# A list scheduler of two MLPs: transfers share one bus in the plan

## The chip, the core and the metric

The kernel runs on one core of a Trainium2 chip. A core has five engines that each carry out their own list of instructions in order: TensorE (PE in the rows; PEld is its loading of weights), VectorE (DVE), ScalarE (ACT), GpSimd (POOL) and SyncE (SP), which here only issues transfers between HBM and the on-chip memory. They wait for one another through semaphores. The metric is the device time of one execution in microseconds.

## The reference, cut to what matters

Two layers over 1024 latent tokens and 256 context tokens of width 1024, all in float32. Layer 0 is windowed attention, layer 1 a gated linear recurrence ("the middle" below); each is followed by a dense MLP:

```
def sqrelu_mlp(h, w1, w2):
    return jnp.square(jax.nn.relu(h @ w1)) @ w2

x = x + mx[2] * rms_norm(y_x, g[1])                       # after the mixer
x = x + mx[5] * rms_norm(sqrelu_mlp(modulate(rms_norm(x, g[2]), mx[3], mx[4]), mlp_w1[i], mlp_w2[i]), g[3])
```

Context tokens go through layer 0's MLP too, not through layer 1's. `mx` are six rows of modulation for each layer, the product of SiLU(c) with `ada_w`. w1 is 1024 x 4096, w2 is 4096 x 1024.

## The kernel before

Float32 products are made of three matmuls on split operands: each operand is a high part, rounded by a cast (line 236), and the remainder (lines 1371, 1465, 1517, 1585); high by high, high by low and low by high are added in a PSUM bank (lines 241 to 243). So each weight or activation tile is loaded, cast and subtracted before TensorE can use it.

The tokens are three groups: 0 and 1 are 512 latent tokens each (tiles 0 to 3 and 4 to 7), 2 is the context (tiles 8 and 9). Layer 0's MLP (`layer0_mlp`) begins with four weight tiles of w1 (`plan_w`, lines 1505 to 1521) by the plain product: the normalized tiles `xn` are loaded, transposed on TensorE (line 1571, tile `ph`), modulated and split (lines 1575 to 1585, tiles `h` and `hf`), then multiplied (`pf`), squared and stored. From then on two weight tiles and both latent groups are done at once by a scheme with seven products in place of eight (`plan_seven`; fourteen steps in layer 0). In a step, TensorE makes p1, p6, p5, p7, p2, p4 and p3 of twelve matmuls each, in banks `al`, `be`, `de`, `ga`; line 1419 (ScalarE) copies p1, line 1421 adds p6, line 1424 adds p7 in bank `ga` and line 1425 p5; p4 adds on in `ga` and p3 in `de`, so they wait for lines 1424 and 1425. Lines 1430 and 1431 make the last two results, lines 1435 and 1437 square them, and they are stored in HBM (`hid_d`). The weights of a step are prepared one step ahead: line 1381 (`s`) and line 1357 are differences and sums of weight blocks, which GpSimd or VectorE can do.

In the second phase (`plan_second`) the hidden tiles are read back and multiplied with w2 in chunks of four hidden tiles (first chunk: two); results are copied (first chunk) or added on (line 1492). Beside layer 0's MLP the modulation rows of the next layer are made on VectorE: a load of 512 KB of `ada_t` (`raw`), and for each one or two products with accumulation (line 1227, operands `raw` and `srow`); when the eight of a row are there, lines 1237 and 317 finish it, and a gate row is then transposed on TensorE (line 325, `gt`).

What sets the order is a planner, the class `Plan`. Each stage adds its operations with an engine (or several to choose from), a duration, a key, what they depend on and which buffers they take and free. `order` goes through them greedily: for each engine it takes the operation with the lowest key among those that can begin about first, on the times that the plan itself keeps, and picks among engines that may do the same work by when they would be done. A transfer is planned with a fixed duration from its issue, any number at once: 2800 ns for a weight tile, 2500 for a tile of activations, 2300 for a store, 3000 for a gate row. `emit` then writes the instructions out in order of planned times, and each engine follows that order on the chip, however long things take there. `KEYS3` holds the numbers of both MLPs; the middle has its own, `KEYS2`, in which there is a key `bw=9` already, for another use. The attention stage's planner uses `KEYS`, the projections `KEYS0`.

Of the kernel before, what the change touches and what calls it, by code (L numbers as in the profile page):

```python
# [42 lines left out]
class Plan:  # L43
# [19 lines left out]
    def any(self, table, order, key, fn, deps=(), take=(), free=(), tab=None):  # L63
        order = order.split()
        return self.add(order, [table[e] for e in order], key, fn, deps, take, free, tab)
# [12 lines left out]
    def order(self):  # L78
        ops = self.ops
        users = [[] for _ in ops]  # L80
        wait = [len(o[3]) for o in ops]
        for i, o in enumerate(ops):
            for d in o[3]:
                users[d].append(i)
        ready = [[] for _ in ops]
        end = {e: self.start.get(e, 0.0) for e in self.LAT}
        open_ = {e: [] for e in self.LAT}
        free = self.free
        tab = None
        for i, o in enumerate(ops):  # L90
            if not wait[i]:
                for e, ns in o[0]:
                    open_[e].append(i)
        at = []
        eps = self.keys["eps"]
        pen = self.keys.get("tab", 0)
        slack = self.keys.get("alt", 0)

        def first(i, e):
            o = ops[i]  # L100
            t = max([end[e]] + [f + self.lat(q, e) for f, q in ready[i]])
            for s in dict.fromkeys(o[4]):
                k = o[4].count(s)
                if len(free[s]) < k:
                    return None
                f = free[s][k - 1]
                t = max(t, f[0] + self.lat(f[1], e))
            return t
        while len(at) < len(ops):
            best = None  # L110
            for e, c in open_.items():
                ts = []
                for i in c:
                    t = first(i, e)
                    if t is None:
                        continue
                    o = ops[i][0]
                    if len(o) > 1 and o[0][0] != e:
                        if t + dict(o)[e] > first(i, o[0][0]) + o[0][1] + slack:
                            continue  # L120
                    ts.append((t, i))
                if not ts:
                    continue
                lim = min(ts)[0] + eps.get(e, 0)
                k, t, i = min((ops[i][1] + (pen if ops[i][6] not in (None, tab) else 0), t, i) for t, i in ts if t <= lim)
                if best is None or t < best[0]:
                    best = t, i, e
            if best is None:
                raise RuntimeError("plan is stuck: " + str([(ops[i][0], ops[i][1], ops[i][4]) for c in open_.values() for i in c]))
            t, i, eng = best  # L130
            opts, key, fn, deps, take, fr, tb, _ = ops[i]
            for e, ns in opts:
                open_[e].remove(i)
            self.got[i] = [(s, free[s].pop(0)[2]) for s in take]
            f = t + dict(opts)[eng]
            if tb is not None and tb != tab and eng == "ACT":
                tab = tb
                f += 1283
            if eng != "DMA":
                end[eng] = f  # L140
            for x in fr:
                s, q = (x, None) if isinstance(x, str) else self.got[x[0]][x[1]]
                free[s].append((f, eng, q))
                free[s].sort(key=lambda x: x[0])
            at.append((t, i, eng, f))
            for u in users[i]:
                ready[u].append((f, eng))
                wait[u] -= 1
                if not wait[u]:
                    for e, ns in ops[u][0]:  # L150
                        open_[e].append(u)
        self.span = max(f for t, i, eng, f in at)
        return at
# [37 lines left out]
class Body:  # L191
    KEYS = {'ctx': 0.706, 'kv': 0.956, 'q': -1.4, 'S': -0.826, 'dS': 0.182, 'v': 0.068, 'e': 0.292, 'n': -0.211, 'tp': 0.197, 'dt': 0.205, 'a': 0.087, 'pv': 0.593, 'o': 0.343, 'w': 0.695, 'dw': 0.162, 'r': 0.664, 'eps': {'ACT': 143.51971938059006, 'Pool': 265}}
    KEYS0 = {'cr': 32.6, 'x': [2.69, 4.49, -4.04, -3.82, 11.07, 11.46, 13.54, 8.52, 59.28, 46.73], 'a0': 6.01, 'ad': 4.7, 'ac': 7.11, 'cp': [1, 0, 0, 0, 1, 1, 0, 1, 1, 1, 1, 1, 0, 1, 0, 0], 'w': [2.18, 62.63, 75.38], 'wd': [13.74, 0.3, 15.36], 'h': [-24.73, 13.55, 40.24], 'hd': [3.18, 5.2, 4.18], 'tl': 19.32, 'blocks': [[[0, 1, 2, 3, 4, 5], [6, 7], [8, 9]], [[0, 1, 2], [3, 4], [5, 6], [7, 8, 9]], [[8, 9, 0], [1], [2], [3]]], 'cq': [1, 0, 0, 1, 0, 1, 0, 1, 1, 1, 1, 0, 0, 0, 0, 1, 1, 0, 1, 1, 0, 1, 1, 1], 'p': [32.68, -6.89, 47.14, 3.71, 20.15, -8.8, 64.94], 'pd': 7.27, 'p1': 82.17, 'qk': -8.12, 'k': 144.05, 'g': [45.38, 61.79, 109.14], 'gd': [5.61, 8.84, 15.66], 'alt': 1800, 'eps': {'Q': 0, 'PE': 0, 'Pool': 44, 'DVE': 27, 'ACT': 0}}
    KEYS3 = dict(r=3, alt=200, eps=dict(DVE=100))
    KEYS2 = dict(m=(2.3, 0.68, 10.54), p=(7.5, 1.52, 9.72), h=(10.4, 11.24, 37.3), pi=0.66, a0=28.64, ap=9.33, al=-5.36, g0=155.5,
                 g1=151.7, gp=4.73, c0=98.5, cp=2.33, w0=312.9, wp=16.6, r0=389.52, spill=5, tab=122.87, alt=72.5, ba=8, bb=6, bw=9, bg=7,
                 bo=0, hm=1, eps=dict(DVE=20, ACT=0, Pool=48))
# [948 lines left out]
    def layer0_mlp(self):  # L1146
        nc, A = self.nc, self.A
        U, l = 4, 0
        dma = nc.sync.dma_start
        p = Plan(self.places(), self.KEYS3, start=dict(PE=9000.0, DVE=5000.0, ACT=5000.0))  # L1150
        self.srow = [None, None]
# [112 lines left out]
    def mlp(self, l, S):  # L1264
# [3 lines left out]
        slots["t"] = [(q, 1) for q in S["free"] + sum(S["hold"], [])]  # L1268
        p = Plan(slots, self.KEYS3)
        hold = [[(p.hold("t", q), 0) for q in v] for v in S["hold"]]  # L1270
# [10 lines left out]


    def plan_second(self, p, l, K, m, n, c, put, last, ys, yop, yh, order, rows=None, fin=False):
        nc, A = self.nc, self.A
        hid, w2, hc = [], [], []
# [12 lines left out]
        for i, t in enumerate(order):  # L1298
# [14 lines left out]
            if fin:  # L1313
                def load(pool, t=t):
                    xs[t] = pool.tile([P, D], F32, tag="x", name=self.name("x"))
                    nc.sync.dma_start(out=xs[t], in_=self.x_d[2, t])
                xop[t] = p.add("DMA", 2500, K, load, [nxt], take=["t"])
                self.plan_residual(p, K + 2 * i + self.KEYS3["r"], t, ys, yop[t], xs, xop[t], G, lambda t, c: nc.sync.dma_start(
                    out=self.out[t, :, c], in_=xs[t][:, c]), False)
# [886 lines left out]
```

## Time and profile before

| | us |
|---|---|
| median of 3 runs (2899.05 to 2900.18) | 2899.95 |
| the profiled execution | 2898.64 |
| its span | 2896.9 |
| TensorE busy in the span | 2685.5 (93%) |
| VectorE busy | 2103.5 (73%) |
| ScalarE busy | 1134.6 (39%) |
| GpSimd busy | 916.2 (32%) |

The attention ends at about 670 us. Layer 0's MLP has its start up to 765, the seven-product steps to 1117 and the second phase to 1525; the middle goes to about 2236, layer 1's MLP has its steps to 2531 and its second phase to 2878, and the rest is the end. Times are from the start of the span. In a row of a timeline the number in brackets is the time for which the engine stood idle just before, and behind the arrow stands what released it. The granted clock (PEclk) is 1.00 at 2.4 GHz and 0.50 at 1.2 GHz.

### The profile page before, as it was taken

Reading aid. Unit: us, or ns where it says so; the run is one execution under the profiler, and the core shown is the slowest. Engines: PE = TensorE matmul, PEld = TensorE weight load, DVE = VectorE, ACT = ScalarE, POOL = GpSimd, SP = SyncE. Lnnn points to the kernel's source line nnn. Section 1 sums busy time; section 2 is a strip of 40 time slices with the busy share of each in tenths; the row PEclk is TensorE's granted clock in tenths of the full one; section 3 lists DMA queues with packets and bytes.
Section 4 is the critical chain, followed back from the end, with each engine's and each line's share of the span. In section 5 each row is a group of like instructions: output and inputs, shape, how many; then the busy total and the mean of one; then the engine's idle time right before and its main releaser. Section 6 shows DMA issues by size and latency. Waiting matters only on the chain.

```text
span 2896.9 us, 35250 instructions
## 1 busy us (share of the span) xinstructions
PE 2685.5 (93%) x12886; PEld 2209.1 (76%) x12886; DVE 2103.5 (73%) x3085; ACT 1134.6 (39%) x2106; POOL 916.2 (32%) x753
## 2 busy tenths in 40 slices
PE   6888999999999999999997998987698999999997
PEld 4676787887788888888885886775576888888886
DVE  8988999996866665655547658689979767655546
ACT  5326777774322223112105335686616222231111
POOL 7653444443311112211106102145628322211113
PEclk9899999999999999999998998998899999999999
DMA  6462321124233335444433213243342233333323
GB/s 235 161 209 92 105 67 59 55 66 167 84 106 113 109 124 176 148 142 138 150 123 145 99 66 109 98 145 125 112 149 95 93 112 117 131 117 116 102 80 123
DMA packets 115332, 345.03 MB, mean 119 GB/s; under 512 B 12836, under 2 KB 15828, under 8 KB 115160
## 3 DMA queue, kind: packets, MB, share of 16 engines
q1 hardware_dynamic: 111704, 330.21, 33.9%
q10 hardware_dynamic: 3456, 12.58, 1.1%
q8 instruction: 101, 1.65, 0.2%
q14 instruction: 71, 0.58, 0.1%
HBM read 254.37 MB, written 88.38 MB: 118 GB/s over the span
## 4 chain that ended last, share of the span: by engine, by line
PE 58%; DVE 18%; issue 8%; ACT 4%; POOL 3%; DMA 2%; SPq 0%; ACTq 0%; DVEq 0%; POOLq 0%
PE py L242 9%; PE py L243 9%; PE py L241 9%; PE pf L243 7%; PE pf L241 7%; PE pf L242 7%; DVE x L1633 2%; PE py L1084 2%; PE tp L1001 1%; PE pv L1015 1%; DVE gi L2079 1%; DVE sc L971 1%; DMA raw<-in_ada_t 1%; DVE gi L2071 1%; PE pq L861 1%
## 5 line engine op out<-in xcount | busy, mean ns | idle before, releaser
L241 PE MATMUL pf<-h,w 128*128 128x512 f32 (+1 forms) x1400 | 520.2, 372 | 23.2 <-DVE c L1424 8.9
L243 PE MATMUL pf<-h,w 128*128 128x512 f32 (+1 forms) x1400 | 518.2, 370 | 13.7 <-DVE w L1517 6.8
L242 PE MATMUL pf<-h,w 128*128 128x512 f32 (+1 forms) x1400 | 518.2, 370 | 7.4 <-DVE h L1585 7.4
L1492 DVE TENSOR_TENSOR y<-y,py 128x512 f32<-128x512 f32 x268 | 180.2, 682 | 258.8 <-PE py L243 258.8
L241 PEld LDWEIGHTS pf<-h,w 128*128 128x128 f32 x1400 | 269.7, 193 | 71.2 <-DVE c L1424 11.4
L243 PEld LDWEIGHTS pf<-h,w 128*128 128x128 f32 x1400 | 269.4, 192 | 60.0 <-POOL w L1517 8.4
L242 PEld LDWEIGHTS pf<-h,w 128*128 128x128 f32 x1400 | 269.5, 193 | 52.9 <-DVE h L1585 10.9
L236 ACT CAST w<-raw 128x1024 fp32r<-128x1024 f32 x132 | 138.4, 1048 | 421.1 <-DMA raw<-in_w 189.2
L236 ACT CAST hw<-raw 128x512 fp32r<-128x512 f32 x159 | 94.1, 620 | 366.0 <-PE py L243 132.1
L241 PE MATMUL py<-hw,hw 128*128 128x512 f32 x608 | 236.6, 389 | 0.8 <-DVE y L1492 0.8
L242 PE MATMUL py<-hw,hw 128*128 128x512 f32 x608 | 236.5, 389 | 0.0
L243 PE MATMUL py<-hw,hw 128*128 128x512 f32 x608 | 236.5, 389 | 0.0
L1465 POOL TENSOR_TENSOR hw<-raw,hw 128x512 fp32r<-128x512 f32 x60 | 90.0, 1507 | 416.3 <-DVE hw L236 257.4
L241 PE MATMUL py<-w,hw 128*128 128x512 f32 x416 | 164.2, 395 | 13.1 <-DVE y L1673 13.1
L995 POOL TENSOR_SCALAR P<-P,sc 128x640 f32<-128x640 f32 (+2 forms) x160 | 118.4, 752 | 179.7 <-DVE sc L992 94.0
L243 PE MATMUL py<-w,hw 128*128 128x512 f32 x416 | 163.3, 393 | 0.0
L242 PE MATMUL py<-w,hw 128*128 128x512 f32 x416 | 163.3, 393 | 0.0
L1084 PE MATMUL py<-w,oT 128*128 128x512 f32 x480 | 146.6, 410 | 2.8 <-DVE w L919 2.1
L1465 DVE TENSOR_TENSOR hw<-raw,hw 128x512 fp32r<-128x512 f32 x144 | 116.2, 837 | 26.4 <-ACT hw L236 26.1
L978 ACT ACTIVATE P<-S,sc 128x640 f32<-128x640 f32 (+2 forms) x160 | 113.9, 712 | 52.7 <-DVE sc L972 37.1
L241 PEld LDWEIGHTS py<-hw,hw 128*128 128x128 f32 x608 | 114.1, 188 | 24.9 <-DVE y L1492 1.3
L243 PEld LDWEIGHTS py<-hw,hw 128*128 128x128 f32 x608 | 114.1, 188 | 23.7
(295 smaller groups left out, 6440.4 us busy)
## 6 DMA issues: line engine op xcount, KB each, us to landing
raw<-in_w SPq DMA_DIRECT2D x128, 512.0 KB, 4.1
raw<-in_ada_t SPq DMA_DIRECT2D x96, 512.0 KB, 4.4
raw<-hid_d SPq DMA_DIRECT2D x64, 512.0 KB, 4.5
hid_d<-c SPq DMA_DIRECT2D x112, 256.0 KB, 2.0
raw<-in_w_in SPq DMA_DIRECT2D x30, 512.0 KB, 4.5
x<-x_d SPq DMA_DIRECT2D x26, 512.0 KB, 4.8
x_d<-x SPq DMA_DIRECT2D x24, 512.0 KB, 2.6
q_d<-qd ACTq DMA_DIRECT2D x20, 512.0 KB, 4.0
```

The source lines that it names most:

```text
L236: (e.copy if e is self.nc.scalar else e.tensor_copy)(out=out, in_=x)
L241: mm(o, lhsT=lh, rhs=rh, start=start, stop=False, skip_group_check=on)
L242: mm(o, lhsT=lh, rhs=rl, start=False, stop=False, skip_group_check=on)
L243: mm(o, lhsT=ll, rhs=rh, start=False, stop=stop, skip_group_check=on)
L861: nc.tensor.matmul(z["ps"], lhsT=self.hview(h, k, t, x), rhs=w[:, y, k % 2], start=m == 0, stop=m == 3 * KT - 1)
L971: nc.vector.tensor_reduce(out=nmx[:, j:j + 1], in_=z["S", j][:, 256:256 + n], op=ALU.max, axis=AX.X, negate=True)
L978: nc.scalar.activation(out=z["P"][j][:, :n], in_=z["S", j][:, 256:256 + n], func=AF.Exp, scale=0.125, bias=negm[:, j:j + 1], accum_out=l[: ...
L995: nc.gpsimd.tensor_scalar(out=z["P"][j][:, :n], in0=z["P"][j][:, :n], scalar1=z["sc"][3][:, j:j + 1], scalar2=1.0, op0=ALU.mult, op1=ALU.mult)
L1084: nc.tensor.matmul(z["ps", n], lhsT=oT[k // 2][2]["oT"][:, x, k % 2], rhs=Wo[k][:, w, n * 512:(n + 1) * 512], start=m == 0, stop=m == 3 * ...
L1465: e.tensor_tensor(out=z[n][:, 1], in0=z["raw"][:, s], in1=z[n][:, 0].bitcast(F32), op=ALU.subtract)
L1492: nc.vector.tensor_tensor(out=y, in0=y, in1=z["ps"], op=ALU.add)
L1633: o.append(p.add("DVE", 665, key, lambda n=n: nc.vector.scalar_tensor_tensor(out=x(n), in0=y(n), scalar=z["a"][:, 2:3], in1=x(n), op0=ALU. ...
```

## The change

`KEYS3` gets a number `bw` (2300 ns). In `order`, a transfer of 2000 ns or more is now also put on a bus: it begins when the bus is free, occupies it for `bw` (half of that if its own duration is up to 2300, as for stores), and is done no sooner than 1500 ns after that. So a load of a weight tile that is alone is planned at 3800 ns from its issue, a store at 2650, and loads that are issued together end 2300 ns one after another. Only the plan's times change; no operation is added or taken away. Since `KEYS2` has a `bw`, the rule also runs in the middle, with 9 ns.

```
@@ Plan.order
         tab = None
+        bus = 0.0
...
             f = t + dict(opts)[eng]
+            if eng == "DMA" and dict(opts)[eng] >= 2000 and self.keys.get("bw"):
+                bus = max(t, bus) + self.keys["bw"] * (1 if dict(opts)[eng] > 2300 else 0.5)
+                f = max(f, bus + 1500)
...
-    KEYS3 = dict(r=3, alt=200, eps=dict(DVE=100))
+    KEYS3 = dict(r=3, alt=200, bw=2300, eps=dict(DVE=100))
```

Behind the inserted lines the line numbers of the kernel are higher: by 1 from line 90 on, by 4 from line 136 on (line 1424 is 1428). TensorE has 12,411 rows in the order before and after, SyncE 764; VectorE goes from 2858 to 2927, ScalarE from 1809 to 1770, GpSimd from 755 to 724, by other choices among engines.

VectorE, the second seven-product step of layer 0 (the one of which rows are shown below), before. `raw` with a number is a loaded tile of `ada_t`, `c_8172` the tile that lines 1421 and 1424 work on:

```order
L1227 SCALAR_TENSOR_TENSOR junk,mod<-raw_8153,srow_7253 128x1024
L1227 SCALAR_TENSOR_TENSOR raw_8153,mod<-raw_8153,srow_7255 128x1024
L1371 TENSOR_TENSOR ws_8193<-s_1453_8189,ws_8193 128x512
L1421 TENSOR_TENSOR c_8172<-c_8172,pf_8176 128x512
L1227 SCALAR_TENSOR_TENSOR junk,mod<-raw_8191,srow_7253 128x1024
L1227 SCALAR_TENSOR_TENSOR raw_8191,mod<-raw_8191,srow_7255 128x1024
L1424 TENSOR_TENSOR c_8224<-c_8172,pf_8196 128x512
L1425 TENSOR_TENSOR c_8224<-c_8224,pf_8157 128x512
L1437 SCALAR_TENSOR_TENSOR c_8224<-c_8224 128x512
```

And after:

```order
L1231 SCALAR_TENSOR_TENSOR junk,mod<-raw_8153,srow_7253 128x1024
L1231 SCALAR_TENSOR_TENSOR raw_8153,mod<-raw_8153,srow_7255 128x1024
L1385 TENSOR_TENSOR s_1455_8204<-raw_7999,raw_8170 128x512
L1425 TENSOR_TENSOR c_8172<-c_8172,pf_8175 128x512
L1375 TENSOR_TENSOR ws_8207<-s_1455_8204,ws_8207 128x512
L1428 TENSOR_TENSOR c_8222<-c_8172,pf_8191 128x512
L1231 SCALAR_TENSOR_TENSOR junk,mod<-raw_8189,srow_7253 128x1024
L1429 TENSOR_TENSOR c_8222<-c_8222,pf_8157 128x512
L1231 SCALAR_TENSOR_TENSOR raw_8189,mod<-raw_8189,srow_7255 128x1024
L1441 SCALAR_TENSOR_TENSOR c_8222<-c_8222 128x512
```

Line 1424 (1428) stood behind both pairs of line 1227 (1231); now it stands behind the first pair alone, and the second pair's rows stand between it, line 1425 (1429) and line 1437 (1441). Line 1381 (1385) has come over from GpSimd. The same is so in each of the six steps with two pairs, of which one had lines 1237 and 317 behind line 1424; those now stand behind line 1437, and the transposes of line 325 on TensorE stand twelve matmuls later, behind p4. In the step that ends the row of steps a pair still stands ahead of line 1424.

VectorE at the end of the attention and the start of layer 0's MLP, before (`y_7160` and `x_7164` are the last tile of the attention's result, `w` the split weight tiles):

```order
L236 CAST w_7277<-raw_7271 128x1024
L236 CAST w_7279<-raw_7273 128x1024
L1517 TENSOR_TENSOR w_7275<-raw_7269,w_7275 128x1024
L1631 TENSOR_TENSOR y_7160<-y_7160,G_3305 128x512
L1517 TENSOR_TENSOR w_7279<-raw_7273,w_7279 128x1024
L1582 TENSOR_SCALAR hf_7313<-ph_7290,mod 128x256
L1631 TENSOR_TENSOR y_7160<-y_7160,G_3305 128x512
L1633 SCALAR_TENSOR_TENSOR x_7164<-y_7160,ss_7166,x_7164 128x512 x2
L236 CAST w_7325<-raw_7284 128x1024
```

After, from the row at which the first weight tile comes:

```order
L1586 TENSOR_SCALAR hf_7369<-ph_7345,mod 128x512
L1586 TENSOR_SCALAR hf_7383<-ph_7350,mod 128x512
L1586 TENSOR_SCALAR hf_7395<-ph_7357,mod 128x512
L1589 TENSOR_TENSOR h_7367<-hf_7383,h_7367 128x512
L1521 TENSOR_TENSOR w_7393<-raw_7269,w_7393 128x1024
L1586 TENSOR_SCALAR hf_7411<-ph_7362,mod 128x512
L1521 TENSOR_TENSOR w_7409<-raw_7271,w_7409 128x1024
L1589 TENSOR_TENSOR h_7407<-hf_7422,h_7407 128x512
L1586 TENSOR_SCALAR hf_7451<-ph_7371,mod 128x512
```

The remainders of the weight tiles (line 1517, now 1521) stood ahead of the last tile's result and the transposed tiles; now they stand behind eight tiles of the context and three of group 0. The three casts of these weight tiles (line 236), one of them on ScalarE and two on VectorE before, are all on ScalarE now, the first behind eight instructions of line 1575 or 1580 (now 1579, 1584) that follow the last tile's line 1645.

TensorE at the same place, before, from the last transposes ahead of the first product:

```order
L1571 MATMUL ph_7343<-ident,xn_7265 128x128
L1571 MATMUL ph_7343<-ident,xn_7267 128x128
L1571 MATMUL ph_7351<-ident,xn_7257 128x128
L1571 MATMUL ph_7351<-ident,xn_7259 128x128
L241 MATMUL pf_7360<-h_7303,w_7275 128x256
L242 MATMUL pf_7360<-h_7303,w_7275 128x256
```

After:

```order
L1575 MATMUL ph_7401<-ident,xn_7261 128x128
L1575 MATMUL ph_7401<-ident,xn_7263 128x128
L1575 MATMUL ph_7401<-ident,xn_7265 128x128
L1575 MATMUL ph_7401<-ident,xn_7267 128x128
L245 MATMUL pf_7415<-h_7290,w_7393 128x256
L246 MATMUL pf_7415<-h_7290,w_7393 128x256
```

Before, 28 single transposes stand ahead of the first product `pf` and the rest among the products; after, 48 do, all of the context and of group 0. From the second group's transposes on, TensorE's order is the same as before. On SyncE, the loads of the fourth weight tile and of the first seven-product step's two, which stood ahead of the tiles `xn` 4 and 5, now stand behind the last `xn` tile.

## Rows read from the trace of the kernel before

**Rows 1.** Busy us by stage: window, length, then PE, PEld, DVE, ACT, POOL.

```profile
765.00:1117.00 352.00, 340.35 (x1803) 292.87 (x1802) 231.16 (x290) 81.39 (x124) 47.92 (x37) 1.00 0.36 121
1117.00:1525.00 408.00, 407.55 (x1799) 337.08 (x1797) 233.51 (x360) 77.79 (x136) 60.55 (x46) 1.00 0.44 144
2262.00:2531.00 269.00, 269.00 (x1187) 222.55 (x1186) 186.68 (x218) 55.13 (x73) 63.42 (x40) 1.00 0.35 120
2531.00:2878.00 347.00, 346.17 (x1527) 286.43 (x1527) 180.24 (x243) 67.66 (x115) 58.68 (x43) 1.00 0.33 107
```

**Rows 2.** Waits of TensorE, 660 to 1120 us: total, times, longest.

```profile
PE pf L241 <- DVE c L1424: 8.9, 6, 2.3
...
PE gt L325 <- DVE mod L317: 2.8, 1, 2.8
```

**Rows 3.** Timeline, TensorE, around two waits: start, us, operation [idle <- releaser].

```profile
791.37 0.39 PE L243 MATMUL pf<-h,w 128*128 128x512 f32 x1
793.03 0.50 PE L241 MATMUL pf<-h,w 128*128 128x512 f32 x1 [1.28 <-DVE c L1424]
793.37 0.40 PE L242 MATMUL pf<-h,w 128*128 128x512 f32 x1
...
1104.86 0.50 PE L241 MATMUL pf<-h,w 128*128 128x512 f32 x1 [0.98 <-DVE c L1424]
```

**Rows 4.** Timeline, VectorE, the same seven-product step.

```profile
785.44 1.23 DVE L1227 SCALAR_TENSOR_TENSOR raw<-raw,srow 128x1024 f32<-128x1024 f32 x1
...
788.50 0.69 DVE L1371 TENSOR_TENSOR ws<-s,ws 128x512 fp32r<-128x512 f32 x1 [1.83 <-ACT ws L236]
...
791.15 1.22 DVE L1227 SCALAR_TENSOR_TENSOR raw<-raw,srow 128x1024 f32<-128x1024 f32 x1
...
792.30 0.68 DVE L1424 TENSOR_TENSOR c<-c,pf 128x512 f32<-128x512 f32 x1
```

**Rows 5.** Timeline, SyncE's queue, GpSimd and ScalarE, the same step.

```profile
786.70 0.33 SPq L220 DMA_DIRECT2D raw<-in_ada_t  x1
...
786.46 1.35 POOL L1381 TENSOR_TENSOR s<-raw,raw 128x512 f32<-128x512 f32 x1 [6.69 <-DMA raw<-in_w]
...
787.85 0.62 ACT L236 CAST ws<-s 128x512 fp32r<-128x512 f32 x1 [6.34 <-POOL s L1381]
```

**Rows 6.** Busy time, 940 to 960 us, around the longest wait.

```profile
940.00:960.00 20.00, 17.25 (x85) 14.33 (x83) 13.34 (x23) 2.55 (x5) 3.32 (x2) 0.91 0.31 112
```

**Rows 7.** Timeline, TensorE, start of the first MLP.

```profile
682.16 0.58 PE L241 MATMUL pf<-h,w 128*128 128x256 f32 x1 [1.95 <-ACT hf L1580]
...
687.87 0.29 PE L242 MATMUL pf<-h,w 128*128 128x256 f32 x1
...
720.35 3.22 PE L1571 MATMUL ph<-ident,xn 128*128 128x128 f32 x28
```

**Rows 8.** Timeline, ScalarE, VectorE and GpSimd, start of the first MLP.

```profile
679.08 1.15 ACT L1645 ACTIVATE y<-x,ss 128x1024 f32<-128x1024 f32 x1 [1.29 <-POOL ss L1625]
...
685.98 2.12 ACT L1575 ACTIVATE h<-ph,mod 128x512 fp32r<-128x512 f32 x3 [1.38 <-PE ph L1571]
...
667.78 3.43 DVE L1517 TENSOR_TENSOR w<-raw,w 128x1024 fp32r<-128x1024 f32 x1
...
671.74 1.21 DVE L1517 TENSOR_TENSOR w<-raw,w 128x1024 fp32r<-128x1024 f32 x1
...
667.27 2.86 POOL L1517 TENSOR_TENSOR w<-raw,w 128x1024 fp32r<-128x1024 f32 x1 [3.44 <-DVE w L236]
```

**Rows 9.** Page, costliest groups: xcount | busy, mean ns | idle before.

```profile
L236 ACT CAST w<-raw 128x1024 fp32r<-128x1024 f32 x132 | 138.4, 1048 | 421.1 <-DMA raw<-in_w 189.2
```

**Rows 10.** Timeline, VectorE, second MLP, first chunk to second.

```profile
2548.42 0.43 DVE L236 CAST hw<-raw 128x512 fp32r<-128x512 f32 x1 [0.34 <-DMA raw<-in_w]
2549.07 1.75 DVE L1465 TENSOR_TENSOR hw<-raw,hw 128x512 fp32r<-128x512 f32 x1 [0.22 <-ACT hw L236]
2554.38 0.69 DVE L1492 TENSOR_TENSOR y<-y,py 128x512 f32<-128x512 f32 x1 [3.56 <-PE py L243]
```

## The prediction, made before the changed kernel was run

> **What bounds the kernel now.** I read four views in this order: the page's busy times, busy time by stage, TensorE's waits, and then the timelines of the few microseconds around each wait. TensorE has by far the most busy time, so a change in the order of work pays only where TensorE stands still or runs at its lower clock. By stage [rows 1]: in the second phase of the first MLP (1117 to 1525 us) it is busy 407.55 of 408.00 us, in the two phases of the second MLP 269.00 of 269.00 and 346.17 of 347.00. Nothing can be won there, only lost. In the seven-product steps of the first MLP (765 to 1117 us) it is busy 340.35 of 352.00: 11.65 us are open. The waits name them [rows 2]: 8.9 us in 6 waits for the VectorE addition of line 1424, and one of 2.8 us for line 317. Ahead of 765 us lies the start of the first MLP, which has stalls too, and which the change also reorders. The middle uses its own key (9 ns in place of 2300) and keeps its order but for a few transfers. So the sum has three terms: the seven-product steps, the start, and the two places where chunks begin.
>
> **Why TensorE waits at line 1424.** Take the step of [rows 3, 4]. TensorE issues a matmul of 512 columns every 0.227 us. The last one of the product p2 starts at 791.37; the next product, p4, adds on in a bank that line 1424 must have read, and starts only at 793.03. VectorE carries out its list in order: two rows of line 1227 on a loaded tile of the next modulation weights (1.23 us each), lines 1371 and 1421, then two more rows of line 1227, the second at 791.15, and only then line 1424 at 792.30. The second tile's load is issued at 786.70 [rows 5], because it goes into the buffer that the first pair frees at 786.67 (785.44 + 1.23). Line 1424 itself needs p7, which ends before p2 begins, twelve matmuls or 2.72 us earlier: about 788.9. So it stands some 3.4 us behind rows that nothing is waiting for. This order recurs in every second step, seven times with the one at line 317 (there the last pair ends a row of modulations, lines 1237 and 317 follow, and the small gate transposes stand ahead of p4 on TensorE).
>
> **The change, term by term.**
>
> *Seven-product steps, gain.* With the new rule a load of 512 KB that has the bus for itself is planned at 2.3 + 1.5 = 3.8 us in place of 2.8. The second tile of line 1227 is thereby expected later, so the greedy plan puts line 1424 ahead of both of its rows in six steps, and moves line 1381 (the difference of two weight blocks) from GpSimd to VectorE, ahead of line 1421. No instruction is added. In the step shown: the first pair ends at 786.67; line 1381 needs the load that GpSimd's row of it began on at 786.46 [rows 5]; on VectorE I give it 0.69 us, as line 1371 on the same shape takes [rows 4]: 787.4. ScalarE's cast of its result (0.62 us [rows 5], and some 0.1 on either side for the hand-over) lies beside line 1421; then line 1371 ends at about 788.9. Line 1424 runs from 789.0 to 789.7, and p4 can start at 791.60, right behind p2: 1.9 us to spare. The next addition, line 1425, now stands behind one row of line 1227 and ends at about 791.9, and p3, which needs it, starts at 794.3. The displaced rows have nobody waiting but the modulation rows of the next layer.
> The six steps: the six waits on line 1424 sum to 8.9, of which the last, 0.98 at 1104.86 [rows 3], I leave (in that step a pair still stands ahead): 7.9. Line 317: 2.75, of which I leave 0.3, since the transposes, now behind p4, come when line 317 is only just done. The bracket of a wait counts from the modelled end of a matmul; the start at 793.03 is 1.43 behind the earliest one (791.37 + 0.23) and not 1.28, and the first spacing after it is 0.34 and not 0.23 [rows 3]: 0.26 more for each, 1.6 for six. Behind the long wait the granted clock of 940 to 960 us is 0.91 [rows 6], which is 3.6 us at the lower level (1.2 GHz), 1.8 us lost; no idle, no loss. Together 7.9 + 2.45 + 1.6 + 1.8 = 13.8 us. Bounds: 14.9 (all of it, the last wait too) and 0 (rival 2).
>
> *Start of the first MLP, loss.* Before, three of the four weight tiles, loaded long ahead, are split in two on ScalarE, VectorE and GpSimd between 666 and 673 us, while the last tile's attention result is finished. Now the plan expects the normalized activations first and puts all 16 transposes of the context and the first group, and ScalarE's and VectorE's work on them, ahead of the splits. TensorE's first product waits for the first split. Walking ScalarE's list: the normalization of the last tile (line 1645) ends at 680.23 [rows 8], which hangs on the attention and stays. Then come eight instructions on transposed tiles, five of 256 columns and three of 512; at 0.71 each, the mean of three on 512 columns [rows 8] and so an upper estimate, 5.7: 685.9. The cast takes 1.05 [rows 9]: 686.95. VectorE's line 1517 takes 1.21 [rows 8]: 688.15. Before, the first product came at 682.16 [rows 7]: 6.0 later. Against that, 20 single transposes that used to stand behind the first product now stand ahead of it, at 3.22 / 28 = 0.115 us [rows 7] worth 2.3. Net 3.7. Bounds: 0 (if ScalarE is through its list as early as the old first product and the transposes' 2.3), and 8 (below). I take 4, nearer to the walk, rounded up since the fourth weight tile's load now also stands on SyncE behind the last activation tile's.
> The far end is in this trace: line 1517 took 3.43 us on VectorE while GpSimd's line 1517, 2.86 us long, ran beside it, and 1.21 us four microseconds later without that [rows 8]. In the new order three such splits stand on VectorE beside five GpSimd instructions of line 1585. Two of them blocked in this way cost 2 x 2.2 = 4.4 on top of the 4: 8.
> The Trainium skill (SBUF — State Buffer, "Who interferes with whom") says that a VectorE instruction with two SBUF inputs contends with a GpSimd instruction that reads SBUF, and that the later of the two waits until the other is through. The 3.43 us row agrees. By that rule the same contention should hit nearly every split at the start, and the sum would have 8 there in place of 4.
>
> *Chunk starts of the second phase, small loss.* More half-tile casts go to VectorE (line 236) and fewer to ScalarE, fewer remainders (line 1465) to GpSimd. In the second MLP the last split ahead of chunk 1 ends at 2549.07 + 1.75 = 2550.8, and the first sum of that chunk is picked up at 2554.38, 2.72 us of matmuls before that means a first matmul at 2551.6 [rows 10]: 0.8 us to spare, and the new list has one cast and one remainder more in that stretch (0.43 [rows 10] and 0.69 as for line 1371 on that shape): 0.3 late, up to 2 if a load is late. In the first MLP the same place has room for several microseconds. I take 0.5, bounds 0 and 3. The loops of later chunks have their splits done with more than half of a chunk to go, in both orders.
>
> Sum against the profiled execution: 2898.64 - 13.8 + 4 + 0.5 = 2889.3. The median of the runs lies 1.3 above the profiled one: **2890.6**.
>
> **Rivals.**
> 1. *The start takes back what the steps give, by the clock: slower.* After the wait of 1.95 us ahead of the first product its matmuls of 256 columns take 0.58 us, and 0.29 from 687.87 on [rows 7]: 5.7 us at the lower level. If the new order, with a longer stop before the first product and a stop at each late split, keeps it there for all of the 38 us up to the second group's transposes at 720.35, the 33 us of work in them at the full clock (38.2 - 2.3 - 2.9) take up to twice as long: a price of up to 30 us over what is slow now. It decides from 20 us on (13.8 gained, 5.8 needed to be told). With 24: 2898.64 - 13.8 + 4 + 0.5 + 24 + 1.3 = 2914.6. For it: the stop is some 4 to 6 us longer. Against it: once the first product runs, 24 matmuls of each split weight tile follow without a new input. A tenth.
> 2. *Line 1381 on VectorE becomes the wait: no change.* It is in order ahead of line 1424 and needs a load. From a start 2 us later than 786.6 on, line 1424 comes late again. If it is so in all six steps, the 13.8 is gone: 2898.64 + 4.5 + 1.3 = 2904.4; if in half of them, 2897.5. For it: GpSimd's copy waited for that very load [rows 5]. Against it: the load is there at 786.46, when the pair has just ended. Two tenths with all mixed cases.
> 3. *The start costs nothing:* 2886.1. One tenth.
>
> The forecast has six tenths. What a measurement of this kernel can tell from no change is about 0.2%, 5.8 us: faster is below 2894.2, slower above 2905.7. The forecast's own spread, 2885 to 2896, lies in faster for nearly all of it; with rival 3 this makes 0.65, rival 2 and the edge of the forecast 0.25, rival 1 0.10. The range, 2885 to 2902, holds the forecast, rival 3 and most of rival 2, and leaves out rival 1 and the worst of 2.
>
> **What would show it.** Gain: the six waits on line 1424 between 765 and 1117 us shrink to one of about 1 us, the wait on line 317 goes, and TensorE is busy above 350 of that stage's 352 us (shorter by 12 to 14). Start: the first product (line 241, now 245) comes at 686 to 689 us, waiting on the split of line 1517 (now 1521), and the second group's transposes at 723 to 726 in place of 720.35. Second MLP: at most 2 us of idle at its first chunk. It is wrong if waits on line 1424 (now 1428) stay, if low-clock matmuls go on after 695 us, or if the second phases lose their full TensorE.

## The result, and the profile after

The changed kernel takes 2881.82 us (median of 4 runs, 2879.99 to 2885.03) against 2900.06 (4 runs, 2899.05 to 2901.84): 0.9938 [0.9920, 0.9955], 18.2 us faster. The forecast was 2890.6, its range 2885 to 2902: the sign was right, and about half of the gain was missing from the sum. Of the executions of before's kernel in the experiments below, one of 6499.94 us, at a granted clock of 0.417, is in no ratio. The profiled execution took 2879.99, its span 2878.2; TensorE is busy for 2680.3 us of it (93%).

The stages of the new trace, as [rows 1] had them:

```profile
765.00:1104.00 339.00, 337.97 (x1805) 293.03 (x1804) 237.89 (x292) 81.31 (x124) 47.95 (x37) 1.00 0.37 127
1104.00:1513.00 409.00, 409.00 (x1808) 338.38 (x1807) 246.03 (x399) 66.13 (x110) 36.16 (x30) 1.00 0.45 144
2245.00:2513.00 268.00, 268.00 (x1184) 221.93 (x1183) 183.55 (x230) 55.22 (x73) 43.49 (x29) 1.00 0.36 119
2513.00:2861.00 348.00, 348.00 (x1537) 288.17 (x1536) 176.90 (x261) 61.00 (x102) 49.55 (x41) 1.00 0.32 106
```

In the seven-product steps TensorE is idle for 1.03 us, where it was for 11.65. Both second phases have none. TensorE's waits from 655 to 1120 us (us in total, times, longest), for [rows 2]:

```profile
PE ph L1575 <- DVE hf L1586: 6.7, 3, 3.9
...
PE gt L329 <- DVE mod L321: 1.0, 1, 1.0
```

No wait on line 1428 (1424 before) is left, not even the one at the end that the prediction left in. What stands in its place in the step of [rows 3, 4] is seen on VectorE (start, us, operation):

```profile
787.91 1.22 DVE L1231 SCALAR_TENSOR_TENSOR raw<-raw,srow 128x1024 f32<-128x1024 f32 x1
...
789.06 0.69 DVE L1385 TENSOR_TENSOR s<-raw,raw 128x512 f32<-128x512 f32 x1
...
790.51 0.69 DVE L1375 TENSOR_TENSOR ws<-s,ws 128x512 fp32r<-128x512 f32 x1 [0.17 <-ACT ws L240]
791.65 0.69 DVE L1428 TENSOR_TENSOR c<-c,pf 128x512 f32<-128x512 f32 x1 [0.45 <-PE pf L247]
792.40 1.23 DVE L1231 SCALAR_TENSOR_TENSOR junk<-raw,srow 128x1024 bf16<-128x1024 f32 x1
```

and on TensorE, the last matmul of p2 and the first of p4:

```profile
793.94 0.39 PE L247 MATMUL pf<-h,w 128*128 128x512 f32 x1
794.17 0.39 PE L245 MATMUL pf<-h,w 128*128 128x512 f32 x1
```

Line 1428 is done at 792.34, 1.8 us before p4's start (the walk had 1.9), and p4 follows at the spacing of 0.23 us. Line 1385, which came over from GpSimd, begins right behind the pair and waits for nothing.

The stages between fixed marks on TensorE (first transposes of layer 0's MLP, second group's transposes, first product of the second phase, its last gate transposes, the middle's first transposes; first product of layer 1's second phase to the end) show where the gain lies. A single trace isn't enough for this: six traces have the same order as before up to the second phase, and they give 444.8 to 448.7 us for start and steps together.

| us | before | after | difference | predicted |
|---|---|---|---|---|
| start of layer 0's MLP (mean of six before) | 49.8 | 50.4 | +0.5 | +4 |
| seven-product steps (mean of six) | 396.6 | 380.9 | -15.6 | -13.8 |
| second phase of layer 0 | 409.0 | 409.0 | 0 | +0.5 for both second phases |
| from it to the middle (mean of three) | 43.9 | 41.9 | -2.0 | not in the sum |
| second phase of layer 1, to the end (eight within 0.1) | 367.1 | 365.1 | -2.1 | in the +0.5 above |

The differences make -19.2; the spans differ by 18.7, the medians by 18.2. The rest of the program (attention up to 670.45 us before and 673.36 after; the middle 664.68 and 661.88) differs about as much between traces of one order: the attention ends at 668.8 to 671.3 in the order before and at 670.99 in a second trace of the order after, and the middle takes 661.8 to 665.3.

### The profile page after: what moved, and what is told of

It is laid out like the page before. It is cut to its first block, busy times and chain, and to the rows that moved or that the text cites. A ratio compares the mean times of both kernels' runs of the same rounds, so it can differ in the third digit from the quotient of the medians.

```text
span 2878.2 us, 35112 instructions
## 1 busy us (share of the span) xinstructions
PE 2680.3 (93%) x12886; PEld 2207.5 (77%) x12886; DVE 2114.9 (73%) x3155; ACT 1116.4 (39%) x2067; POOL 855.6 (30%) x722
## 4 chain that ended last, share of the span: by engine, by line
PE 64%; DVE 17%; issue 4%; ACT 3%; POOL 2%; DMA 2%; SPq 0%; DVEq 0%; ACTq 0%; POOLq 0%
PE py L246 9%; PE py L247 9%; PE py L245 9%; PE pf L247 9%; PE pf L246 9%; PE pf L245 9%; DVE x L1637 2%; PE py L1088 2%; DVE gi L2083 1%; PE tp L1005 1%; PE pv L1019 1%; DVE sc L975 1%; DVE gi L2075 1%; DVE pt L1012 1%; DVE h L1589 1%
## 5 line engine op out<-in xcount | busy, mean ns | idle before, releaser
L240 ACT CAST hw<-raw 128x512 fp32r<-128x512 f32 x127 | 76.9, 621 | 365.1 <-DMA raw<-in_w 146.8
L1469 POOL TENSOR_TENSOR hw<-raw,hw 128x512 fp32r<-128x512 f32 x44 | 66.7, 1517 | 484.6 <-DVE hw L240 302.4
L245 PEld LDWEIGHTS py<-hw,hw 128*128 128x128 f32 x608 | 114.1, 188 | 23.8
L246 PEld LDWEIGHTS py<-hw,hw 128*128 128x128 f32 x608 | 114.1, 188 | 23.6
L247 PEld LDWEIGHTS py<-hw,hw 128*128 128x128 f32 x608 | 114.1, 188 | 23.6
```

The costliest lines, as they stand in the source:

```text
L240: (e.copy if e is self.nc.scalar else e.tensor_copy)(out=out, in_=x)
L245: mm(o, lhsT=lh, rhs=rh, start=start, stop=False, skip_group_check=on)
L246: mm(o, lhsT=lh, rhs=rl, start=False, stop=False, skip_group_check=on)
L247: mm(o, lhsT=ll, rhs=rh, start=False, stop=stop, skip_group_check=on)
L1469: e.tensor_tensor(out=z[n][:, 1], in0=z["raw"][:, s], in1=z[n][:, 0].bitcast(F32), op=ALU.subtract)
```

## The experiments

Before's own single times go from 2890.2 to 2905.5 over these runs, so each verdict rests on a ratio with its interval, and on the stages of its trace. Unless told otherwise, the kernel is before's, and the rule on the bus holds only for transfers with keys in a part of the program, or for one of the MLPs. The edit of the first one; the others have other bounds in `bus`, or have it in the plan of layer 1's MLP:

```
+            if eng == "DMA" and dict(opts)[eng] >= 2000 and self.keys.get("bus") and self.keys["bus"][0] <= key < self.keys["bus"][1]:
+                bus = max(t, bus) + self.keys["bw"] * (1 if dict(opts)[eng] > 2300 else 0.5)
+                f = max(f, bus + 1500)
...
-        p = Plan(self.places(), self.KEYS3, start=dict(PE=9000.0, DVE=5000.0, ACT=5000.0))
+        p = Plan(self.places(), dict(self.KEYS3, bus=(-1e12, 80)), start=dict(PE=9000.0, DVE=5000.0, ACT=5000.0))
```

**Each part alone.** Start of layer 0's MLP, keys below 80:

> The bus is in the plan only for the transfers of layer 0's MLP that belong to its start (keys under 80); every other transfer is planned as before. Theory A (the terms of the prediction): the start alone costs time, 4 us (bounds 0 and 8): ratio 1.0014, about 2904. Theory B (the trace after: second group's transposes 50.4 us behind the first transposes, in place of 49.9): the start costs 0 to 1 us, since the longer stop is made up by matmuls at the higher clock: ratio 1.0000 to 1.0003. Theory C: the reordered start itself brings part of the 18 us: ratio 0.998 or less.

Measured: 1.0012 [1.0003, 1.0020], +3.5 us. The number is near the sum's 4, but this is not the start of the whole change. In the changed kernel 192 products `pf` stand ahead of the second group's transposes, here 144; the other 48 come behind the first products of the seven-product steps, so the marks of the table do not part the same work. Behind 372 products, ahead of the first step's 48 of 256 columns, every order has done the same work: this trace is there 103.1 us behind the first transposes, the six in the order before 100.9 to 102.2, the changed kernel 101.4. From there to the second phase it takes 347.5, those six 343.1 to 346.8, with the old waits at about the same size. So it does not tell what the change's own start costs; the last two experiments do.

```profile
PE pf L245 <- DVE c L1428: 9.3, 6, 2.2
PE ph L1575 <- DVE hf L1586: 6.4, 3, 3.9
```

The seven-product steps, keys from 80 up to 900:

> The bus is in the plan only for the transfers of layer 0's seven-product steps (keys 80 to 900). Theory A: the six waits on line 1424 and the one on line 317 go, 13.8 us: ratio 0.9952, about 2886. Theory B: the same 14 us, and nothing else changes behind them. Theory C (the gain in the steps is given back later, or the steps bring all of it): ratio above 0.998, or 0.9938 as the whole change.

Measured: 0.9948 [0.9936, 0.9961], -15.1 us; start and steps 431.9 in place of 446.4, -14.5. This part carries four fifths of the gain.

The second phase of layer 0, keys from 900 on:

> The bus is in the plan only for the transfers of the second phase of layer 0's MLP (keys from 900 on). Theory A: nothing or up to 0.5 us lost: ratio 1.0000 to 1.0002. Theory B (the trace after: the first waits of the middle on line 1673 are 13.1 us before and 10.9 after, the stage is reached 2.7 us earlier): 2 to 4 us gained by other choices at the end of the second phase: ratio 0.9987 to 0.9993. Theory C: those 2.7 us only follow from when the clock and the transfers happen to stand, so alone it brings 0.

Measured: 0.9974 [0.9964, 0.9985], -7.5 us. The phase itself is unchanged (408.97); between it and the middle the trace has 41.45 in place of 43.9. So there is a term behind the phase that the sum did not have. Its 2.5 us are less than the whole interval allows (4.3 to 10.4); the remainder isn't settled.

Layer 1's MLP:

> The bus is in the plan only for layer 1's MLP. Theory A: 0 to 0.5 us lost: ratio 1.0000 to 1.0002, with up to 2 us of idle at its first chunk. Theory B (the trace after: 2.7 us less from the middle's end to the end): 2 to 3 us gained, of which about 1 behind the last matmul: ratio 0.9990 to 0.9993. Theory C: those microseconds belong to the middle's end and to chance: ratio 1.0000.

Measured: 0.9988 [0.9980, 0.9997], -3.5 us. No stall where its chunks begin, and 2.1 us less in its second phase and the end (365.1).

The rule only in the middle; every engine's list is then the same as before:

```
+            if eng == "DMA" and dict(opts)[eng] >= 2000 and self.keys.get("bw") == 9:
```

> The new rule works in the middle alone, with its 9 ns; both MLPs are planned as before. All five engines' lists are those of the kernel before. All theories: ratio 1.0000. What it measures is how far two traces of one program lie apart, stage by stage: theory A, that the 2.9 us by which the attention is longer in the trace after, and the 2.8 by which the middle is shorter, are such differences; theory B, that they are not (then this trace has both stages within 0.5 us of the trace before).

Measured: 0.9998 [0.9989, 1.0008]. The same instructions gave 398.68 us for the steps and 49.98 for the start, with the waits

```profile
PE pf L245 <- DVE c L1428: 9.1, 6, 2.3
...
PE gt L329 <- DVE mod L321: 3.9, 1, 3.9
```

so 1 to 3 us between two traces, in one stage, are no evidence.

**What in the plan does it.** No bus; only the loads of `ada_t` are planned longer:

```
-                o = p.add("DMA", 2800, key, load, [dep], take=["raw"])
+                o = p.add("DMA", 4300, key, load, [dep], take=["raw"])
```

> The kernel before, without a bus; only the loads of the modulation weights are planned at 4.3 us from their issue in place of 2.8. In the six steps line 1424 then stands ahead of the second pair of line 1227, as in the changed kernel; line 1381 stays on GpSimd, and the start and layer 1's MLP stay as before. Theory A (line 1424 behind the second pair is the whole loss in the steps): 13 to 15 us gained, ratio 0.9950 to 0.9955. Theory B (line 1381 on VectorE has a part in it): half of that, 0.9975. Theory C: the bus itself, loads one behind another, is needed: 1.0000.

Measured: 0.9961 [0.9947, 0.9974], -11.3 us; start and steps 433.5, -12.9. TensorE's waits:

```profile
PE gt L325 <- DVE mod L317: 1.8, 1, 1.8
PE pf L241 <- DVE c L1424: 0.8, 1, 0.8
```

Of 8.9 us on line 1424, 0.8 is left: one planned duration makes most of the gain. And no bus, but all loads planned at 3.8 us and all stores at 2.65:

```
+                f = max(f, t + self.keys["bw"] * (1 if dict(opts)[eng] > 2300 else 0.5) + 1500)
```

> The changed kernel without the sharing: each load is planned at 3.8 us and each store at 2.65 us from its issue, any number at once. Theory A (what counts is the length of one load in the plan, not the queue on the bus): about the whole gain in the steps (13 to 15 us), the rest depends on how the start and the chunks fall out: ratio 0.993 to 0.996. Theory B (the sharing matters in the second phases, where loads come in fours): 0.9948 at best, the 8 to 10 us of the second phase and of layer 1's MLP are lost.

Measured: 0.9933 [0.9921, 0.9945], -19.4 us; start and steps 428.6. That transfers stand behind one another in the plan is not needed; a longer planned load is enough. In both of these runs line 1381 is still on GpSimd in the six steps.

**The start inside the whole change.** The changed kernel, without the bus in the start (nor in the middle, where the rule changes no list):

```
+        p = Plan(self.places(), dict(self.KEYS3, bus=(80, 1e12)), start=dict(PE=9000.0, DVE=5000.0, ACT=5000.0))
```

> The changed kernel with the bus taken out of the plan for the start of layer 0's MLP alone (keys under 80): the weight tiles are split ahead of the transposes again. Theory A (the start costs 3 to 4 us, as it does alone): 3 to 4 us less than the changed kernel, ratio to the kernel before 0.9925. Theory B (the trace after: start and steps together take 431.3 us after and 431.9 with the steps alone): the same as the changed kernel, 0.9938.

Measured: 0.9923 [0.9911, 0.9936], 2876.98. Its trace has 430.2 for start and steps, that of the whole change 431.3. The two intervals overlap.

**Between second phase and middle.** Before's kernel, in which the middle's loads of `x` for groups 0 and 1 are planned 3 us later. On the chip this changes SyncE's order alone: the loads of the first two weight tiles now stand ahead of these loads.

```
-                xop[t] = p.add("DMA", 2500, kp[g] + i, load_x(t, 0), [hid[0, g]["op"]], take=["t"])
+                late = p.when([hid[0, g]["op"]], [], 3000) if g != 2 else None
+                xop[t] = p.add("DMA", 2500, kp[g] + i, load_x(t, 0), [hid[0, g]["op"], late], take=["t"])
```

> The kernel before, in which only the middle's loads of the residual tiles x (groups 0 and 1) are planned 3 us later. Every engine's list stays as before but SyncE's: the middle's first weight load now stands ahead of the x loads that stood ahead of it. Theory A (the traces so far: the stretch from the gate transposes to the middle's first transposes is 44.0 us where that weight tile is cast 8.0 us behind the transposes, and 41.5 where it is cast 5.2 behind): the stretch comes down to 41.5 to 42.5, ratio 0.9990 to 0.9994. Theory B (the second phase's other choices on VectorE and ScalarE make the stretch shorter, the load's place does not matter): no change, 1.0000.

Measured: 0.9986 [0.9977, 0.9996], -4.1 us; between second phase and middle 38.87 in place of 43.9. Three timelines, of SyncE's queue and of ScalarE, tell it. Before:

```profile
1521.18 3.96 SPq L1717 DMA_DIRECT2D x<-x_d  x3
1525.88 0.28 SPq L328 DMA_DIRECT2D g_d<-gr  x1
...
1526.60 0.42 SPq L220 DMA_DIRECT2D raw<-in_w_in  x1
...
1533.29 1.05 ACT L236 CAST w<-raw 128x1024 fp32r<-128x1024 f32 x1 [4.88 <-DMA raw<-in_w_in]
1538.39 1.05 ACT L236 CAST w<-raw 128x1024 fp32r<-128x1024 f32 x1 [4.05 <-DMA raw<-in_wg]
```

The changed kernel:

```profile
1508.27 3.72 SPq L1721 DMA_DIRECT2D x<-x_d  x3
1514.27 0.28 SPq L332 DMA_DIRECT2D g_d<-gr  x1
...
1514.98 0.42 SPq L224 DMA_DIRECT2D raw<-in_w_in  x1
...
1519.50 1.05 ACT L240 CAST w<-raw 128x1024 fp32r<-128x1024 f32 x1 [2.70 <-DMA raw<-in_w_in]
1524.61 1.05 ACT L240 CAST w<-raw 128x1024 fp32r<-128x1024 f32 x1 [4.06 <-DMA raw<-in_wg]
```

And this experiment:

```profile
1526.56 0.34 SPq L220 DMA_DIRECT2D raw<-in_w_in  x1
1527.46 0.33 SPq L220 DMA_DIRECT2D raw<-in_wg  x1
1527.84 4.10 SPq L1717 DMA_DIRECT2D x<-x_d  x6
...
1531.42 1.05 ACT L236 CAST w<-raw 128x1024 fp32r<-128x1024 f32 x1 [2.67 <-DMA raw<-in_w_in]
1533.47 1.05 ACT L236 CAST w<-raw 128x1024 fp32r<-128x1024 f32 x1 [1.00 <-DMA raw<-in_wg]
```

The load of the first weight tile of the middle, from its issue to the cast that it releases, takes 6.7 us before, 4.5 after the change and 4.9 here. In the 2.3 us ahead of its issue two loads of `x` are issued before, and one in each of the other two. The stretch hangs on the cast behind it, that of the second tile (`in_wg`): counted from the gate transposes it starts at 13.1, 11.0 and 7.9 us, and in all fourteen traces the middle's first transposes come 30.8 to 31.0 us behind it. Behind this cast stand, in ScalarE's list, the sums of squares (line 1617, now 1621) that VectorE's next rows wait for. So the changed kernel gains 2.2 us by the first tile, and this experiment 2.2 by the first and 3.1 more by the second. TensorE's waits for line 1673 (1677), the addition that empties the banks of the second phase's last products, fall with it. Before, from 1525 to 1570 us:

```profile
PE py L241 <- DVE y L1673: 13.1, 5, 4.6
```

the changed kernel, 1513 to 1557:

```profile
PE py L245 <- DVE y L1677: 10.9, 5, 4.1
```

this experiment, 1525 to 1566:

```profile
PE py L241 <- DVE y L1673: 9.0, 4, 4.7
```

The same edit with the third part's bus:

> The bus in the plan for the second phase of layer 0's MLP alone (as e3), and the middle's x loads planned 3 us later (as e5). Theory A (what the second phase's bus gains is the place of the middle's first weight load, which e5 alone moves too): the same as e5, ratio 0.9980 to 0.9988, and a stretch from the gate transposes to the middle's first transposes of 38 to 39 us. Theory B (the second phase's bus gains something else, 3 us or more, which the traces don't show): 0.9960 to 0.9972.

Measured: 0.9973 [0.9962, 0.9983], -7.8 us; between second phase and middle 37.52. The second tile's cast starts 6.5 us behind the gate transposes, so this stretch too is as short as its weight tiles are early. The ratio lies between the two expectations and decides neither: whether the bus in the second phase gives something outside of this stretch is open.

**The best of both.** The changed kernel with the loads of `x` planned later, by the same two lines (and with the rule for `bw` above 9 alone, so not in the middle):

> The changed kernel whole, with the same x loads planned 3 us later; it differs from e9 by the start alone. Theory A (the start costs 3.5 us, as alone): ratio 0.0012 above e9. Theory B (inside the whole change it costs 1 us or nothing, by the traces: start and steps 431.3 against 430.2 us): within 0.0004 of e9.

Measured: 0.9917 [0.9902, 0.9932], 2874.28; between second phase and middle 37.51. And without the bus in the start as well, the two edits of the last two parts together:

> The bus in the plan without the start (as e8) and the middle's x loads planned 3 us later (as e5). Theory A (the two gains are apart from each other: 22 us in e8, and the stretch behind the second phase at 41.2 us there against 38.9 in e5): 2 us more than e8, ratio 0.991 to 0.992. Theory B (the middle's first weight load is early in e8 already): the same as e8, 0.9923.

Measured: 0.9911 [0.9895, 0.9927], 2873.44 against 2896.56, the fastest here. It is 0.8 us from the run above, less than either interval: inside the whole change the start can't be told from free.

## Why the forecast was right, and where it was wrong

The stages' differences sum to -19.2, the three terms to -9.3. Of the 9.9 us between them, the start makes 3.5, layer 1's second phase with the end 2.6, the stretch ahead of the middle 2.0 and the steps 1.8.

**Seven-product steps: right.** The mechanism is the one predicted: a load of `ada_t` that the plan expects later puts line 1424 ahead of rows that nobody waits for. The gain was 15.6 where the sum had 13.8 with a bound of 14.9; by before's own trace alone it is 14.9, and six traces of that order differ by 3.9, so the 1.8 on top are not clear of noise. The waits of [rows 2] alone, 8.9 and 2.8, would have made 11.7, less the 1.0 that is left 10.7; so the terms for the restart (1.6) and the lower level of the clock (1.8) belong in the sum. Rival 2, line 1381 as the new wait, did not come: 0.17 us ahead of line 1375 is all. That line plays no part in the gain either: with it on GpSimd, longer loads without a bus give steps of 381.3, the changed kernel 380.9.

**Start: the failed term, +4 where +0.5 came.** The walk to the first product was about right. It came 16.4 us behind the first transposes in place of 11.7 (682.16 in [rows 7] less 670.45): +4.7, where the walk had 6.0. What failed was the other side, 2.3 us for the transposes that move ahead, as all that the products behind the first one gain. TensorE in the changed kernel:

```profile
684.75 5.38 PE L1575 MATMUL ph<-ident,xn 128*128 128x128 f32 x24 [1.89 <-DVE hf L1586]
689.78 0.56 PE L245 MATMUL pf<-h,w 128*128 128x256 f32 x1
...
690.72 0.28 PE L246 MATMUL pf<-h,w 128*128 128x256 f32 x1
...
723.73 3.22 PE L1575 MATMUL ph<-ident,xn 128*128 128x128 f32 x28
```

From the first product to the second group's transposes 33.95 us pass, where it was 38.19: 4.2 less, of which 1.9 are not the moved transposes. A second trace of the new order gives 16.43 and 33.94. In [rows 7] TensorE waited 1.95 us right ahead of the first product, and then ran matmuls of 256 columns at 0.58 us for 5.7 us. Now 24 transposes stand between the wait and the first product, without a pause; they run at 0.224 each (0.115 is their pace at the full clock), and 0.9 us into the products the matmuls are down to 0.28. Busy time from the first product on before (682 to 720), and after from 673 to 690 and from 690 to 724, with the granted clock in the third column from the right:

```profile
682.00:720.00 38.00, 37.84 (x211) 34.06 (x212) 20.58 (x27) 15.74 (x28) 11.96 (x9) 0.92 0.29 110
...
673.00:690.00 17.00, 10.10 (x52) 8.66 (x51) 11.58 (x19) 12.60 (x25) 8.39 (x10) 0.72 0.85 329
690.00:724.00 34.00, 34.00 (x196) 30.04 (x196) 19.67 (x20) 11.79 (x21) 10.88 (x8) 0.99 0.29 101
```

The stretch at the lower level (1.2 GHz) did not go; it fell on work that had to be done anyway ahead of the products, while the stop was taken up by it. The prediction kept that stretch on the products and added a full 4 us. Rival 1 took the clock for the danger, the forecast for a constant; rival 3, that the start costs nothing, is near to what came: +0.5 in the table, +1.2 against three traces with the new steps and the old start (49.1 to 49.2), 0.8 between the last two experiments. The sign that the prediction gave for its loss, the second group's transposes at 723 to 726, came (723.73) by luck: the attention ended 2.9 us later in this trace.

The far end of this term, 8 us, was put on splits that are blocked beside GpSimd. VectorE in the changed kernel has them, with GpSimd's rows at the same time:

```profile
688.50 1.22 DVE L1521 TENSOR_TENSOR w<-raw,w 128x1024 fp32r<-128x1024 f32 x1
...
691.06 2.13 DVE L1521 TENSOR_TENSOR w<-raw,w 128x1024 fp32r<-128x1024 f32 x1 [0.63 <-ACT w L240]
...
694.44 1.81 DVE L1521 TENSOR_TENSOR w<-raw,w 128x1024 fp32r<-128x1024 f32 x1
...
688.06 4.05 POOL L1589 TENSOR_TENSOR h<-hf,h 128x512 fp32r<-128x512 f32 x2
693.88 1.29 POOL L1824 TENSOR_TENSOR hf<-hf,hf 128x512 f32<-128x512 f32 x1 [1.76 <-DVE h L1589]
```

Two of the three take 0.9 and 0.6 longer than 1.22, but behind the first one TensorE has 24 matmuls to do for each, and does not wait. The rule of the Trainium skill (SBUF — State Buffer, "Who interferes with whom") that the prediction weighed agrees with these rows: each of the two ends some 1.1 us after the GpSimd instruction beside it (692.11 and 695.17). It cost the sum nothing, and the far end of the term was not needed.

**Middle: the step that failed by being left out.** "The middle uses its own key (9 ns in place of 2300) and keeps its order but for a few transfers. So the sum has three terms." SyncE's order is indeed the same before and after in the rows above; its times are not, and no term stood for them. Between second phase and middle TensorE waits, on a chain that hangs on when the middle's first two weight tiles are there. This brought 2.0 us here; with the loads of `x` moved behind both tiles, it brought 5.0 of trace. It does not take the bus in the second phase: the start alone and the steps alone have 42.1 and 42.8 there. [Rows 1] show full stages, and none of the four stages takes in 1525 to 1570.

**Chunk starts: -2.1 where +0.5 was put.** The answer to [rows 10]:

```profile
2534.45 1.06 DVE L240 CAST hw<-raw 128x512 fp32r<-128x512 f32 x1 [0.37 <-DMA raw<-in_w]
2535.55 1.34 DVE L1469 TENSOR_TENSOR hw<-raw,hw 128x512 fp32r<-128x512 f32 x2
2537.78 0.69 DVE L1496 TENSOR_TENSOR y<-y,py 128x512 f32<-128x512 f32 x1 [0.89 <-PE py L247]
```

The first sum comes at 2537.78, and 2.72 us of matmuls before it means a first matmul at 2535.1, without a wait. The two remainders of the rows end at 2536.9, behind that, so the chunk does not wait for them; the walk took VectorE's last split ahead of the sum for what the chunk needs, and here it is not. What was gained is at the other end, where the prediction didn't look. VectorE before:

```profile
2887.09 2.41 DVE L1633 SCALAR_TENSOR_TENSOR x<-y,ss,x 128x512 f32<-128x512 f32 x2
2889.43 0.67 DVE L1492 TENSOR_TENSOR y<-y,py 128x512 f32<-128x512 f32 x1
```

and after:

```profile
2865.66 2.40 DVE L1637 SCALAR_TENSOR_TENSOR x<-y,ss,x 128x512 f32<-128x512 f32 x2
2867.99 1.87 DVE L1496 TENSOR_TENSOR y<-y,py 128x512 f32<-128x512 f32 x3
```

Before, one addition of the last ones is done there, with its fellows placed elsewhere; after, three stand together. About half of the 2.1 lies in the end (18.10 to 17.17 us), half in the phase (349.06 to 347.93), where before had a wait of 0.83 us on line 1492 at 2877.49. All five traces with the bus there have these 2.1 us, and the eight with before's plan there don't, so the bus there causes them (longer loads without a bus give 0.9); that these rows are the way is read, not tested.

## What to carry to other kernels

Where a list is made from planned times and then carried out in order, the planned duration of a transfer decides who stands behind whom: one that was too short put work that nobody waits for ahead of an addition that TensorE needed, and cost 15 us. Price the whole critical engine, the stretches between stages too, before an effect is called small; full stages say nothing about the seams. Here the stretch at the lower clock stayed with what followed the stop, 24 transposes in place of the products, so ask what a new order puts behind a stop.

## What had not been expected of the chip

One list of instructions gave 395.87 and 398.68 us for the same steps in two executions, and a burst of 25 transposes in the middle, always behind a wait of 1.5 to 1.9 us, took 4.6 us in four traces (before among them, at a granted clock of 0.62) and 2.95 in ten. The load of the middle's first weight tile took 6.1 to 6.9 us from issue to cast in the six traces with two loads of `x` issued in the 2.3 us ahead of it, and 4.2 to 4.9 in the eight with one or none.
